# Two dense tiles of the latent tokens in one PSUM bank: layer 1's mixer of a hybrid backbone kernel

## The chip, the cores and the metric

The kernel runs on one core of one Trainium2 chip. The metric is the device time of one launch in microseconds (us), the median of several runs. Three runs of the kernel before took 2468.72, 2463.49 and 2462.4 us: median 2463.49.

## What is computed

Two layers work on 256 latent tokens and 256 context tokens of width 1024, in fp32. Each layer normalises, projects its input, runs three mixers side by side (centred pooling, a bidirectional RWKV-7 recurrence, neighbourhood attention), projects each mixer's output, gates and sums the three, and projects again; then comes a feed-forward part, dense in layer 0 and with 8 experts in layer 1. In the last layer the context is only read: it needs its keys, values and recurrence inputs, but no outputs. The reference, cut to the mixer:

```python
def token_mixer(h, hc, w_in, ..., need_ctx_out):
    zp, zr, zq, zk, zv, zg = jnp.split(h @ w_in, splits, axis=-1)
    zrc = hc @ w_in[:, OFF_RWKV:OFF_Q]                  # last layer: of the context only these
    zkc, zvc = jnp.split(hc @ w_in[:, OFF_K:OFF_GATE], 2, axis=-1)
    ...
    branches = (pool_branch(zp, ...), rwkv_readout(wkv, ...), nat)
    y = gated_merge(branches, zg, w_branch, w_out)

def gated_merge(branches, gate_pre, w_branch, w_out):
    proj = jnp.einsum('btnc,ncd->btnd', jnp.stack(branches, axis=2), w_branch)
    gates = jax.nn.sigmoid(gate_pre.reshape(B, T, N_BRANCH, D_MODEL))
    return jnp.sum(gates * proj, axis=2) @ w_out
```

## The kernel before

Activations lie transposed, channels on the 128 partitions, tokens along the free axis: the context's 256 columns, then the latent 256. A *dense tile* is 128 output channels: one tile of weights (128 x 1024, or 128 x 512 for a branch projection) is loaded, ScalarE casts it to a high part `whi` (L205), VectorE subtracts to get a low part `wlo` (L209), and TensorE adds up three products for each of 8 (or 4) blocks of the input: `whi` with the input's high part, `whi` with its low part, `wlo` with its high part, 24 (or 12) matmuls into one PSUM tile (L249 to L251, or L499 to L501 where other work is woven in between). There are two `whi`/`wlo` buffers for the mixer's weights, so the cast for the tile after next waits until TensorE has used up the first.

A dense tile's PSUM comes from `mm`, which in the mixer has two banks of 512 fp32 columns (`self.psum(f"m{l}", sm=2, mm=2)`). In layer 0 all tiles have 512 columns, context and latent. In layer 1 (`full` is False) the tiles that the context doesn't need, pooling inputs, r, the recurrence's gate input `glo`, queries, the 24 output gates, the branch projections and the output projection, have only the latent 256; such a tile takes a bank and uses half of it:

```python
def bank(self, tag, n):
    p, bufs = self.banks[tag]
    t = p.tile([128, 512], F32, name=tag, tag=tag, bufs=bufs)
    return t[:, :n]
```

A bank goes to the next tile when the last instruction that reads it is done. These readers *empty* a tile: a ScalarE copy for pooling inputs (L1205), for queries and keys (L1085) and values (L1116); ScalarE with a scale and then VectorE twice for r, k, v and `glo`, which are shifted by a token both ways (L531, L533, L535); ScalarE's Tanh for a gate (L1257); VectorE for a branch projection, multiplied with its gate (L1269 in the woven part, L1246 in the last merge); VectorE's residual for the output projection (L1521). They are given a high priority (`leave()`).

Order: up to the end of the recurrence's readout TensorE's order is written out. `Order.run` takes pieces of several lanes (attention, triangular solves, norms) by due times, and dense tiles fill what is left. TensorE runs its instructions in that order, whatever is ready. The other engines' order is set by the scheduler. In layer 1 the mixer has four stages:

- the front: k, r, v, pooling, queries, keys, values of w_in, and the recurrence's operands;
- attention (`attend`), the triangular solves (`solve`) and, as filling, `pool_merge`: for f = 0 to 7 a gate tile (24 matmuls), then a merge tile (12 matmuls) of the pooling branch; then four `early_gate` tiles, gates of the recurrence's branch;
- the chunk scan (`core`), 8 chunks in both directions, with `dense` as filling: per f a gate tile of the recurrence's branch (for f = 4 to 7; the first four are there), a gate tile and a merge tile of the attention branch;
- the last merge of the recurrence's branch (`merge_branch`, 8 tiles of 12) and the output projection (8 tiles of 24, with routing products L1646 for the experts). Here the scheduler orders TensorE too.

Then come the experts, fed from HBM.

Of the kernel before, what the change touches and what calls it, by code (L numbers as in the profile page):

```python
# [54 lines left out]
class Order:  # L55
# [4 lines left out]
    def __init__(self):  # L60
        self.now, self.lanes = 0.0, []
# [42 lines left out]
class Builder:  # L104
    def __init__(self, ctx, tc, I, out, dbg=None):
        self.ctx, self.tc, self.nc, self.I, self.out = ctx, tc, tc.nc, I, out
        self.dbg = dbg or {}
        self.nlo, self.lo_first = 0, 0
        self.pre, self.ahead = [], []
        self.raws, self.parted, self.pin = (), (), False  # L110
        self.late_lo = ()
        self.nraw = self.nparts = 0
        self.banks = {}
        self.norm_banks = ExitStack()
        self.sq = self.rs = None
        self.hw = 512
        self.cpool = ctx.enter_context(tc.tile_pool(name="consts", bufs=1))
        self.dram = ctx.enter_context(tc.tile_pool(name="dr", bufs=1, space=DRAM))
        nc = self.nc
        cst = self.cpool.tile([128, C_N], F32, name="cst")  # L120
        nc.sync.dma_start(cst, I["cst"])
        self.cst = cst
        self.ident = cst[:, C_ID:C_ID + 128]
        self.mask = cst[:, C_MSK:C_MSK + 128]
        self.i2 = cst[:, C_I2:C_I2 + 64]
        self.ob = cst[:, C_OB:C_OB + 128]
        self.ones = cst[:, C_ON:C_ON + 128]
        self.tiny = ctx.enter_context(tc.tile_pool(name="tiny", bufs=6))
        hb = self.cpool.tile([40, 4, 128], F32R, name="hb")
        with tc.tile_pool(name="hb0", bufs=1) as hp:  # L130
            hb0 = hp.tile([40, 4, 128], F32, name="hb0")
            nc.sync.dma_start(hb0, I["heads"])
            nc.vector.tensor_copy(hb, hb0)
        self.hb = hb
        self.vec = []
        for l in range(2):
            v = self.cpool.tile([128, V_N], F32, name=f"vec{l}")
            nc.sync.dma_start(v, I["vec"][l])
            self.vec.append(v)
        self.mod = [[None] * 6 for _ in range(2)]  # L140
# [35 lines left out]
        return t[:, :n]  # L176

    def mm(self, n=512):
        return self.bank("mm", n)

    def sm(self, n=512):
        return self.bank("sm", n)
# [1090 lines left out]
    def mixer(self, l, x, full, xnew, done=lambda: None):  # L1273

        nc, tc = self.nc, self.tc
        n = 512 if full else 256
# [4 lines left out]
        n = 512 if full else 256  # L1281
        self.bonus, self.gain = ([self.dram.tile([128, n], F32, name=f"{a}{l}{c}") for c in range(4)] for a in ("bon", "gan"))
        ex = ExitStack()
        P = lambda name, bufs, **k: tc.tile_pool(name=f"{name}{l}", bufs=bufs, reuse_waits="tile", **k)
        ex.enter_context(self.psum(f"m{l}", sm=2, mm=2))
        self.sp_small = ex.enter_context(P("small", 1))
        self.lo_mod, self.lo_pool, self.lo_first = 2, 0, 0
        self.raws, self.parted = (self.wa, self.wa) + tuple(ex.enter_context(P("w", 1)) for _ in range(l)), (self.wa,)
# [372 lines left out]
    def moe(self, l, x):  # L1661
        nc, tc, I = self.nc, self.tc, self.I
        ident = self.ident
        with ExitStack() as ex:
            P = lambda name, bufs, **k: ex.enter_context(
                tc.tile_pool(name=f"{name}m", bufs=bufs, reuse_waits="tile", **k))
            ex.enter_context(self.psum("e", mm=4))
            self.lo_mod, self.lo_pool = 8, 0
            self.nlo, self.lo_first = 0, 0
            self.nparts, self.parted = 0, (P("w", 2), self.wa)  # L1670
# [464 lines left out]
```

## Time and profile before

| | |
|---|---|
| median of three runs | 2463.49 us |
| the profiled execution | 2462.03 us, span 2459.8 us |
| TensorE (PE) busy | 2310.2 us, 94% of the span |
| weight loads (PEld) busy | 1851.1 us, 75% |
| VectorE (DVE) busy | 1894.2 us, 77% |
| ScalarE (ACT) busy | 1281.2 us, 52% |
| GpSimd (POOL) busy | 95.4 us, 4% |
| DMA | 514.29 MB, mean 209 GB/s |

Times of the rows below count from the span's start. A busy matmul is not one at its peak, since matmuls overlap. "Idle before" is the time for which an engine had nothing running ahead of the instruction, and what ended it; a wait for several things is put down to the last. The mixer of layer 1 ends at about 1645 us, the experts take the rest.

### The profile page before, as it was taken

The page shows a single profiled execution, that of the slowest core. Times are in us where ns is not written, and L with a number is a line of the kernel's source. Part 1 is how long each engine was busy: PE and PEld are TensorE (multiplying, and loading weights), DVE is VectorE, ACT ScalarE, POOL GpSimd, SP SyncE. Part 2 cuts the span into 40 slices and gives each one's busy share as a digit, 9 for nine tenths or more (in the row PEclk, how much of TensorE's full clock was granted, in tenths as well). Part 3 has the DMA queues.
Part 4 walks back from the last instruction along what each step waited for, and adds up shares of the span by engine and source line. Part 5 has one row for each costly group of instructions (what it writes and reads, how often), then busy time and mean ns, then how long its engine had stood idle before and what let it go on. Part 6 is the DMA issues. An engine that isn't in the chain of part 4 may idle for free. (4 is left out here: it accounts for less than half of the span.)

```text
span 2459.8 us, 40024 instructions
## 1 busy us (share of the span) xinstructions
PE 2310.2 (94%) x15206; PEld 1851.1 (75%) x15206; DVE 1894.2 (77%) x3133; ACT 1281.2 (52%) x1882; POOL 95.4 (4%) x94
## 2 busy tenths in 40 slices
PE   6899998999899999999889898889999999999998
PEld 4667667777578888777667687678888888888876
DVE  4795776787857666765885867769999999889897
ACT  4563654222333322234654543258777777777775
POOL 0000000000001221120000000000000000000000
PEclk9999998999999999999989989989999999999999
DMA  6274223564424444762663345576999999999995
GB/s 254 87 199 124 91 90 92 173 179 151 150 86 137 152 140 138 265 207 78 167 166 107 112 130 172 168 273 221 366 339 346 362 359 337 348 360 338 358 345 194
DMA packets 227594, 514.29 MB, mean 209 GB/s; under 512 B 70875, under 2 KB 105051, under 8 KB 226243
## 3 DMA queue, kind: packets, MB, share of 16 engines
q1 hardware_dynamic: 227394, 511.67, 61.7%
q8 instruction: 121, 1.98, 0.3%
q14 instruction: 79, 0.64, 0.1%
HBM read 484.79 MB, written 26.74 MB: 208 GB/s over the span
## 5 line engine op out<-in xcount | busy, mean ns | idle before, releaser
L205 ACT CAST whi<-wraw 128x1024 fp32r<-128x1024 f32 (+2 forms) x753 | 755.0, 1020 | 601.1 <-DMA wraw<-in_ffn 185.9
L209 DVE TENSOR_TENSOR wlo<-wraw,whi 128x1024 fp32r<-128x1024 f32 (+1 forms) x719 | 838.9, 1193 | 169.8 <-ACT whi L205 158.6
L499 PE MATMUL mm<-h,whi 128*128 128x512 f32 (+1 forms) x864 | 344.9, 399 | 24.1 <-ACT u L1085 6.7
L501 PE MATMUL mm<-h,wlo 128*128 128x512 f32 (+1 forms) x864 | 318.1, 368 | 7.6 <-DVE wlo L209 7.6
L500 PE MATMUL mm<-h,whi 128*128 128x512 f32 (+1 forms) x864 | 318.9, 369 | 4.9 <-DVE h L484 4.9
L1853 PE MATMUL mm<-whi,xh 128*128 128x512 f32 (+1 forms) x768 | 289.2, 377 | 0.0
L1854 PE MATMUL mm<-whi,xl 128*128 128x512 f32 (+1 forms) x768 | 288.1, 375 | 0.0
L1855 PE MATMUL mm<-wlo,xh 128*128 128x512 f32 (+1 forms) x768 | 281.5, 376 | 1.3 <-DVE wlo L209 1.3
L499 PEld LDWEIGHTS mm<-h,whi 128*128 128x128 f32 x864 | 171.0, 198 | 76.4 <-issue 24.6
L501 PEld LDWEIGHTS mm<-h,wlo 128*128 128x128 f32 x864 | 171.0, 198 | 37.5 <-DVE wlo L209 11.3
L500 PEld LDWEIGHTS mm<-h,whi 128*128 128x128 f32 x864 | 171.9, 199 | 31.5 <-DVE h L484 8.0
L251 PE MATMUL mm<-h,wlo 128*128 128x512 f32 (+1 forms) x448 | 171.4, 383 | 2.2 <-DVE wlo L209 2.0
L250 PE MATMUL mm<-h,whi 128*128 128x512 f32 (+1 forms) x448 | 170.3, 381 | 0.7 <-DVE h L484 0.7
L249 PE MATMUL mm<-h,whi 128*128 128x512 f32 (+1 forms) x448 | 169.7, 381 | 1.4 <-ACT whi L205 1.4
L1855 PEld LDWEIGHTS mm<-wlo,xh 128*128 128x128 f32 x768 | 144.0, 188 | 29.2 <-DVE wlo L209 1.9
L1854 PEld LDWEIGHTS mm<-whi,xl 128*128 128x128 f32 x768 | 144.4, 188 | 27.1
L1853 PEld LDWEIGHTS mm<-whi,xh 128*128 128x128 f32 x768 | 144.6, 188 | 26.4
L1882 PE MATMUL mm<-wlo,hh 128*128 128x512 f32 x352 | 139.6, 397 | 0.8 <-DVE wlo L209 0.8
L1881 PE MATMUL mm<-whi,hl 128*128 128x512 f32 x352 | 139.1, 395 | 0.0
L1880 PE MATMUL mm<-whi,hh 128*128 128x512 f32 x352 | 138.8, 394 | 0.0
L209 POOL TENSOR_TENSOR wlo<-wraw,whi 128x1024 fp32r<-128x1024 f32 (+1 forms) x34 | 79.4, 2337 | 760.7 <-DMA wraw<-in_ffn 426.6
L251 PEld LDWEIGHTS mm<-h,wlo 128*128 128x128 f32 x448 | 84.5, 189 | 22.3 <-DVE wlo L209 3.3
(378 smaller groups left out, 3751.9 us busy)
## 6 DMA issues: line engine op xcount, KB each, us to landing
wraw<-in_moe SPq DMA_DIRECT2D x516, 512.0 KB, 5.5
wraw<-in_w_in SPq DMA_DIRECT2D x108, 512.0 KB, 3.7
wraw<-in_w_mod SPq DMA_DIRECT2D x72, 512.0 KB, 4.6
wraw<-in_ffn SPq DMA_DIRECT2D x60, 512.0 KB, 3.7
rakbv<-std SPq DMA_DIRECT2D x32, 640.0 KB, 5.3
wraw<-in_w_branch SPq DMA_DIRECT2D x48, 256.0 KB, 2.7
u<-in_w_mod SPq DMA_DIRECT2D x48, 256.0 KB, 4.3
std<-st SPq DMA_DIRECT2D x16, 640.0 KB, 5.2
```

Source lines behind the costliest of these rows:

```text
L205: nc.scalar.copy(hi, src)
L209: return e.tensor_tensor(lo, src, hi.bitcast(F32), op=OP.subtract)
L249: nc.tensor.matmul(ps, wh, xh, start=i == 0, stop=False)
L250: nc.tensor.matmul(ps, wh, xl, start=False, stop=False)
L251: nc.tensor.matmul(ps, wl, xh, start=False, stop=i == n - 1)
L499: nc.tensor.matmul(ps, wh, xh, start=i == 0, stop=False)
L500: nc.tensor.matmul(ps, wh, xl, start=False, stop=False)
L501: nc.tensor.matmul(ps, wl, xh, start=False, stop=i == n - 1)
L1853: nc.tensor.matmul(ps, xh[:, k0 + k], hi[:, w], start=k0 + k == 0, stop=False)
L1854: nc.tensor.matmul(ps, xl[:, k0 + k], hi[:, w], start=False, stop=False)
L1855: nc.tensor.matmul(ps, xh[:, k0 + k], lo[:, w], start=False, stop=k0 + k == 7)
L1882: nc.tensor.matmul(y, hid[k][0], lo[:, w], start=False, stop=k == KF - 1)
```

## The change

`mm` gets a mode, `pairs`, switched on for the mixer of layer 1 and off for the experts. With it a tile of at most 256 columns takes a new bank only every second time: the first takes columns 0 to 255, the next one columns 256 to 511 of the same bank. A tile of more than 256 columns takes a bank of its own and ends an open pair.

```diff
--- before.py
+++ after.py
@@ -106,6 +106,7 @@
         self.ctx, self.tc, self.nc, self.I, self.out = ctx, tc, tc.nc, I, out
         self.dbg = dbg or {}
         self.nlo, self.lo_first = 0, 0
+        self.pairs, self.half = False, None
         self.pre, self.ahead = [], []
         self.raws, self.parted, self.pin = (), (), False
         self.late_lo = ()
@@ -176,7 +177,15 @@
         return t[:, :n]
 
     def mm(self, n=512):
-        return self.bank("mm", n)
+        if n > 256 or not self.pairs:
+            self.half = None
+            return self.bank("mm", n)
+
+        if self.half is None:
+            self.half = t = self.bank("mm", 512)
+            return t[:, :256]
+        t, self.half = self.half, None
+        return t[:, 256:]
 
     def sm(self, n=512):
         return self.bank("sm", n)
@@ -1283,6 +1292,7 @@
         ex = ExitStack()
         P = lambda name, bufs, **k: tc.tile_pool(name=f"{name}{l}", bufs=bufs, reuse_waits="tile", **k)
         ex.enter_context(self.psum(f"m{l}", sm=2, mm=2))
+        self.pairs, self.half = not full, None
         self.sp_small = ex.enter_context(P("small", 1))
         self.lo_mod, self.lo_pool, self.lo_first = 2, 0, 0
         self.raws, self.parted = (self.wa, self.wa) + tuple(ex.enter_context(P("w", 1)) for _ in range(l)), (self.wa,)
@@ -1665,6 +1675,7 @@
             P = lambda name, bufs, **k: ex.enter_context(
                 tc.tile_pool(name=f"{name}m", bufs=bufs, reuse_waits="tile", **k))
             ex.enter_context(self.psum("e", mm=4))
+            self.pairs, self.half = False, None
             self.lo_mod, self.lo_pool = 8, 0
             self.nlo, self.lo_first = 0, 0
             self.nparts, self.parted = 0, (P("w", 2), self.wa)
```

In the new file the lines of the mixer stand nine or ten further down: L499 becomes L508, L1257 becomes L1266, L1269 becomes L1278, L1646 becomes L1656.

What the change does to the order shows in three places. The number of a buffer tells which allocation it is; `[waits ...]` names the engine whose count the instruction waits for. First, TensorE in the attention stage, where merge 1 ends and gate 2 begins; then two score products of attention (`sm`) and one of the recurrence's output gate. Before:

```order
L500 MATMUL mm_12013<-u2_11799,whi_12009 128x256
L501 MATMUL mm_12013<-u2_11798,wlo_12010 128x256
L499 MATMUL mm_12040<-h_10011,whi_12036 128x256 [waits Activation_49]
L500 MATMUL mm_12040<-h_10012,whi_12036 128x256
L501 MATMUL mm_12040<-h_10011,wlo_12037 128x256 [waits DVE_49]
L1150 MATMUL sm_12045<-u_11571,u_11150 128x512
L1150 MATMUL sm_12046<-u_11571,u_11150 128x512 [waits Activation_49]
L764 MATMUL sm_12073<-u_11859,g2_10116 128x256 [waits DMAHW3_49,Activation_49]
L499 MATMUL mm_12040<-h_10020,whi_12036 128x256
```

and now:

```order
L509 MATMUL mm_12007<-u2_11795,whi_12003 128x256
L510 MATMUL mm_12007<-u2_11794,wlo_12004 128x256
L508 MATMUL mm_12007<-h_10011,whi_12030 128x256 [waits DVE_49]
L509 MATMUL mm_12007<-h_10012,whi_12030 128x256
L510 MATMUL mm_12007<-h_10011,wlo_12031 128x256
L1159 MATMUL sm_12038<-u_11567,u_11148 128x512
L1159 MATMUL sm_12039<-u_11567,u_11148 128x512 [waits Activation_49]
L773 MATMUL sm_12066<-u_11855,g2_10116 128x256 [waits DMAHW3_49,Activation_49]
L508 MATMUL mm_12007<-h_10020,whi_12030 128x256
```

The order is the same; gate 2 now goes to the bank of merge 1, and its first matmul waits for VectorE, where it waited for ScalarE. Its third matmul has no wait for `wlo` of its own any more.

Second, ScalarE at the start of the scan: casts of weights, and the Tanh of the last early gate and of the first gate of `dense` (`u_13434` before, `u_13420` now). Before:

```order
L205 CAST whi_13469<-wraw_13467 128x512
L1257 ACTIVATE gp_13066<-mm_13073 128x256
L205 CAST whi_13491<-wraw_13489 128x1024
L1257 ACTIVATE u_13434<-mm_13441 128x256
L205 CAST whi_13551<-wraw_13549 128x512
```

and now:

```order
L214 CAST whi_13455<-wraw_13453 128x512
L1266 ACTIVATE gp_13053<-mm_13013 128x256
L214 CAST whi_13476<-wraw_13474 128x1024
L1266 ACTIVATE u_13420<-mm_13427 128x256
L214 CAST whi_13536<-wraw_13534 128x512
```

Nothing moves here: the cast for the tile after next stands ahead of the Tanh in both.

Third, TensorE in the output projection, at the end of its first tile (f=0, then the routing product `nl` of f=0). Before:

```order
L250 MATMUL mm_15712<-h_15676,whi_15706 128x256 [waits DVE_49]
L251 MATMUL mm_15712<-h_15675,wlo_15707 128x256
L250 MATMUL mm_15750<-h_15676,whi_15744 128x256
L251 MATMUL mm_15750<-h_15675,wlo_15745 128x256
L249 MATMUL mm_15712<-h_15702,whi_15706 128x256 [waits Activation_49]
L249 MATMUL mm_15750<-h_15702,whi_15744 128x256
L250 MATMUL mm_15712<-h_15703,whi_15706 128x256 [waits DVE_49]
L251 MATMUL mm_15712<-h_15702,wlo_15707 128x256
L250 MATMUL mm_15750<-h_15703,whi_15744 128x256
L251 MATMUL mm_15750<-h_15702,wlo_15745 128x256
L1646 MATMUL nl_15475<-xl_10270,rt1_15463 8x256 [waits DVE_49]
L1646 MATMUL nl_15475<-xl_10272,rt1_15463 8x256 [waits DVE_49]
```

and now:

```order
L258 MATMUL mm_15684<-h_15674,whi_15678 128x256 [waits Activation_49]
L259 MATMUL mm_15684<-h_15675,whi_15678 128x256 [waits DVE_49]
L260 MATMUL mm_15684<-h_15674,wlo_15679 128x256
L1656 MATMUL nl_15451<-xl_10270,rt1_15439 8x256 [waits DVE_49]
L258 MATMUL mm_15684<-h_15493,whi_15716 128x256
L259 MATMUL mm_15684<-h_15494,whi_15716 128x256
L260 MATMUL mm_15684<-h_15493,wlo_15717 128x256
L258 MATMUL mm_15684<-h_15519,whi_15716 128x256
L259 MATMUL mm_15684<-h_15520,whi_15716 128x256
```

Before, f=0 (`mm_15712`) and f=1 (`mm_15750`) are worked on in turn; now the whole of f=0 stands ahead of the first matmul of f=1, and so does its routing product, which waits for VectorE.

## Rows read from the trace of the kernel before

**Rows 1.** Windows by stage: length, then busy (count) of each engine.
```profile
core 0: us, PE busy (x) PEld busy (x) DVE busy (x) ACT busy (x) POOL busy (x), PEclk, DMA share, GB/s
1186.00:1317.00 131.00, 111.88 (x788) 89.32 (x788) 101.03 (x173) 72.55 (x130) 3.94 (x14) 0.91 0.62 162
1317.00:1455.00 138.00, 122.74 (x1252) 102.90 (x1251) 100.92 (x234) 70.36 (x129) 0.31 (x1) 0.89 0.35 108
1455.00:1592.00 137.00, 122.36 (x1942) 107.97 (x1940) 98.81 (x226) 47.34 (x100) 0.00 (x0) 0.98 0.57 170
1592.00:1645.00 53.00, 47.75 (x324) 40.25 (x324) 34.17 (x70) 25.05 (x51) 0.00 (x0) 0.91 0.75 280
1660.00:2459.00 799.00, 788.01 (x3818) 653.76 (x3816) 722.03 (x743) 603.58 (x675) 1.81 (x1) 1.00 0.90 329
```

**Rows 2.** TensorE's waits, 1317 to 1455: us in total, times, longest.
```profile
PE mm L501 <- DVE wlo L209: 5.2, 8, 1.4
PE mm L499 <- ACT u L1257: 2.8, 3, 1.3
```

**Rows 3.** TensorE's waits, 1455 to 1592.
```profile
PE sm L877 <- issue: 4.6, 4, 1.9
PE sm L877 <- DVE Gr L883: 3.3, 4, 1.0
```

**Rows 4.** TensorE's waits, 1186 to 1317.
```profile
PE mm L499 <- ACT u L1085: 6.7, 2, 4.2
PE mm L499 <- ACT z L1205: 5.3, 2, 3.1
```

**Rows 5.** Timeline, first gate and merge of the scan: start, length, instruction.
```profile
1453.64 0.41 PE L501 MATMUL mm<-h,wlo 128*128 128x256 f32 x1
1453.85 0.41 PE L499 MATMUL mm<-u,whi 128*128 128x256 f32 x1
1453.92 1.05 ACT L205 CAST whi<-wraw 128x1024 fp32r<-128x1024 f32 x1 [2.73 <-issue]
...
1454.88 0.38 ACT L1257 ACTIVATE u<-mm 128x256 f32<-128x256 f32 x1
```

**Rows 6.** Timeline, last gate and merge of the scan.
```profile
1563.55 0.28 PE L499 MATMUL mm<-u,whi 128*128 128x256 f32 x1
...
1564.20 0.38 ACT L1257 ACTIVATE u<-mm 128x256 f32<-128x256 f32 x1
```

**Rows 7.** Timeline, attention: from merge 1 to gate 2.
```profile
1333.56 0.38 PE L499 MATMUL mm<-h,whi 128*128 128x256 f32 x1 [0.62 <-ACT u L1257]
...
1334.61 0.38 PE L501 MATMUL mm<-h,wlo 128*128 128x256 f32 x1 [0.55 <-DVE wlo L209]
...
1334.84 0.42 DVE L1269 SCALAR_TENSOR_TENSOR u<-u,mm 128x256 f32<-128x256 f32 x1
```

**Rows 8.** Timeline, attention: gate 0 starts; the glo tile is emptied.
```profile
1321.25 0.39 PE L499 MATMUL mm<-h,whi 128*128 128x256 f32 x1
...
1323.31 0.48 DVE L535 SCALAR_TENSOR_TENSOR u<-mm,vec,u 128x255 f32<-128x255 f32 x1
```

**Rows 9.** Timeline, attention: early gate 3 starts; early gate 2 is emptied.
```profile
1428.45 0.28 PE L499 MATMUL mm<-h,whi 128*128 128x256 f32 x1
...
1430.27 0.39 PE L501 MATMUL mm<-h,wlo 128*128 128x256 f32 x1 [1.42 <-DVE wlo L209]
...
1432.26 0.37 ACT L1257 ACTIVATE gp<-mm 128x256 f32<-128x256 f32 x1
```

**Rows 10.** Timeline, output projection: f=0 and f=1 are emptied; f=2 starts.
```profile
1620.20 0.88 DVE L1521 SCALAR_TENSOR_TENSOR xl<-mm,mod,xl 128x256 f32<-128x256 f32 x2 [1.84 <-PE mm L251]
...
1621.70 0.39 PE L249 MATMUL mm<-h,whi 128*128 128x256 f32 x1
```

**Rows 11.** Two windows of the attention stage; columns as in rows 1.
```profile
1411.00:1413.30 2.30, 1.43 (x9) 1.22 (x10) 2.25 (x7) 2.30 (x6) 0.00 (x0) 1.00 0.00 0
1413.40:1416.70 3.30, 3.30 (x24) 2.76 (x23) 1.35 (x2) 0.65 (x2) 0.00 (x0) 0.50 0.74 264
```

## Prediction

> **What bounds the kernel now.** I read the stage windows first, since the edit lives in one stage, layer 1's mixer, and what it is worth there decides; then the waits of TensorE in that stage; then the order of instructions of both programs; last the timeline at the places that the order marks. The windows [rows 1] cut the mixer into its front (1186 to 1317 us), attention with the pooling merges (to 1455), the chunk scan with the attention merges (to 1592) and the last merge with the output projection (to 1645). TensorE is busy 111.88 of 131, 122.74 of 138, 122.36 of 137 and 47.75 of 53 us: it is the bound, with 5 to 19 us of idle per stage. The experts behind it keep TensorE busy 788.01 of 799 us, so they can't make up what the mixer loses: a microsecond there is a microsecond at the end.
>
> How much of that idle time is the lack of a free `mm` bank, which is what the change speaks to? In attention TensorE waited 2.8 us in all, three times, for ScalarE to empty a gate tile (L1257) [rows 2]; in the scan no `mm` wait is among the long ones [rows 3]; in the front it waited 6.7 us for L1085 and 5.3 us for L1205 [rows 4]. That is 14.8 us, the most that more tiles in flight could give.
>
> **What the change does in the order.** A pair shares one bank, and in the built program the first matmul of the right half carries a wait for the instruction that empties the left half (first place in the order: before, gate f+1 waited for ScalarE, for a tile two back; now for VectorE, for merge f's L1269, numbered L1278 in the new file). So not four tiles are in flight but two, one per bank, and the neighbour in a pair is the tile just behind, not two behind. I count the second halves of the mixer: 4 in the front, 10 in attention, 10 in the scan, 4 in the last merge, 4 in the projection. In the front three of the four wait for the same emptying as before, since there the scheduler already put the tile into the bank just emptied (the other was held by a 512-column tile); so the 12.0 us of [rows 4] stay, and one wait is new. 29 new waits in all. TensorE works in order, so all behind the waiting matmul on it waits too: scores, transposes and the scan's products, and with them the VectorE and ScalarE work that those feed.
>
> A rule speaks to this. The Trainium skill's page "PSUM — Partial Sum Buffer", section "PSUM bank collisions raise a hardware error", says that the hardware neither arbitrates nor stalls when two engines touch one bank and quadrant, even at different addresses, and that PSUM is to be guarded by bank, not by address. No run here shows a collision; by that rule no schedule could drop these waits.
>
> **The price of one wait**, from the timeline of before: the end of the emptying instruction, plus 0.05 us to the first matmul, less the time at which the second tile started, less the idle time behind it that goes because its own cause has passed meanwhile.
> - Scan, first: the gate's last matmul starts at 1453.64, the merge's first at 1453.85, and the gate's Tanh runs 1454.88 to 1455.26 [rows 5]. The merge would start at 1455.31: 1.46 us later. The Tanh isn't late by chance: ScalarE first casts the weights of the tile after next (1.05 us from 1453.92), into the buffer that the gate's last matmuls free, and this order is the same in both programs (second place). 0.44 us of later idle (a wait for VectorE's `wlo`) goes: 1.0.
> - Scan, last: 1563.55 against a Tanh that ends at 1564.58 [rows 6]: 1.1.
> - Between them eight more, read likewise: 1.7, 1.2, 1.1, 1.0, 1.8, 1.5, 0.7, 0.8. Ten together: 11.7. TensorE also idled 4.6 us before L877, four times, for nothing that the profile shows [rows 3]; late in the scan that may be a `rakbv` transfer that would then arrive in time. I take 2 off: 9.7.
> - Attention, gate behind merge (five): merge 1 is emptied by L1269, 1334.84 to 1335.26, and gate 2 would start at 1335.31. In before it started at 1333.56, ran two matmuls and then stood until 1334.61 for `wlo` [rows 7]. `wlo` is ahead of L1269 on VectorE, so that stand goes: 0.70 later, plus the two matmuls, 0.95. The five: 1.0, 0.95, 0.6, 0.6, 0.9, together 4.1.
> - Attention, the others: gate 0 behind the glo tile, whose last reader L535 ends at 1323.79, against a start at 1321.25 [rows 8]; three `rh` products (0.43 us each) now stand ahead of it, 1.3 left. Merges 6 and 7 behind their gates 0.8 and 1.1. Early gate 1: 1.9. Early gate 3: its neighbour is emptied at 1432.63, it started at 1428.45 and lost 1.42 us at 1430.27 anyway [rows 9]: 2.5. Together 7.6, attention 11.7.
> - Front: one wait at the scan's price, 1.5.
> - Last merge and projection have no hand-written order. There the right half can't run beside the left any more: projection tiles f=0 and f=1 were interleaved (third place in the order) and both emptied in 1620.20 to 1621.08, with f=2 at 1621.70 [rows 10]. Now f=1 starts when f=0 is emptied, about 1620.7, and its 24 matmuls at some 0.12 us (0.21 at half clock [rows 5]) take 2.9: f=2 comes at 1623.5, 1.8 late. Three more pairs at about 0.6 (emptying 0.48, less the routing product between): 1.8. The first pair of the merge loses its overlap likewise, twelve matmuls and 0.42: 1.9. Together 5.5.
>
> No instruction is added or removed; the DMAs are the same and only shift with their buffers.
>
> Sum: 1.5 + 11.7 + 9.7 + 5.5 = 28.4 us of waiting.
>
> **The clock.** TensorE's granted clock fell from its level of 2.4 GHz (share 1.00) to 1.2 (0.50) behind idle times no longer than these: in 1411.0 to 1413.3 it was busy 1.43 of 2.30 us at 1.00, and in 1413.4 to 1416.7 it ran at 0.50 [rows 11]. Such a stretch of 3.3 us does 1.65 us of full-speed work and so costs 1.65. But the scan, with 14.6 us of idle time in 137, kept a mean of 0.98 [rows 1]. 29 idle times of about 1 us bring some: with three, 5.0 us. None is the lower bound, one behind every second wait (14, 23 us) the upper.
>
> So 28.4 + 5.0 = 33.4. The profiled execution took 2462.0 us (span 2459.8), 1.5 below the median of 2463.5; on the median that is **2497 us**. Bounds: the emptying can come sooner than I read it, for TensorE's standing gives the other two engines time to catch up (the latest, at 1432.63 [rows 9], sat behind other ScalarE work). With 0.5 us left per wait, 29 make 15: 2478. With nothing absorbed (5 us in the scan and behind `wlo` more) and eight slow stretches, 28.4 + 5 + 13 = 46, and a few more for knock-on waits: 2515.
>
> **The rivals.**
> - *The halves do work side by side* (the other side: faster). If the right half were written while the left is emptied, the 14.8 us of [rows 2, 4] would go at most: 2449. For it: these waits are real, and they sit on the engine that bounds. The Trainium skill's page "Perfetto Trace Analysis", section "Optimization Strategy", says that the same gap repeating on the engine that should be saturated can mean too little PSUM for the next tile; [rows 4] look like that, and by it the change would be the cure. Against: the waits stand in the built order, and in the front the same tiles wait for the same emptyings. It decides only if most second halves start before the left is emptied. 4 in 100.
> - *Nothing to measure*: gains in the front and losses behind cancel, 2460 to 2470. 5 in 100.
> - *The waits are there but short*: eviction is prompt once TensorE stands, about 0.35 us left for each, no clock loss: 10 us, 2473. For it: L1521 runs at once behind its tile [rows 10]; against: the cast ahead of each Tanh [rows 5] waits for the same matmuls as the Tanh. 9 in 100.
> - *The clock pays most*: a slow stretch behind two of three waits, 20 x 1.65 = 33 more: 2525. For it [rows 11]; against, the scan's 0.98. 9 in 100.
>
> **Numbers.** The likeliest, 2484 to 2512 around 2497, has 73 in 100. The range 2478 to 2515 leaves out the faster and same cases, part of the short waits and most of the clock case. A change of under 0.3%, 7.4 us, can't be told from none here: faster 0.04, same 0.05, slower 0.91.
>
> **What would show it.** In the profile after, the waits list of TensorE in attention and scan gets new entries: gate matmuls of L499 (there L508) waiting for L1269's successor L1278, and merge matmuls waiting for the Tanh L1266, about ten each way, mean near 1.3 us, before absorption. The `wlo` waits of [rows 2] shrink. The projection's f=0 and f=1 come one after the other. The expert stage keeps its length, about 799 us from its first weights. More half-clock stretches in 1317 to 1592. Wrong would be: no such entries; or entries that sum to under 15 us; or the extra time in the experts.

## The result, and the profile after

The changed kernel took 2494.95 us (median of 4 runs: 2492.51, 2491.53, 2497.40, 2497.76), the kernel before beside it 2462.97. Ratio 1.0123, 95% interval 1.0099 to 1.0147: slower. 2497 was predicted, 2478 to 2515 the range.

The profiled execution took 2492.51 us (span 2490.3, 30.5 more than before). The windows of the changed kernel that answer to [rows 1], cut at the same tiles:

```profile
1191.40:1322.00 130.60, 112.11 (x788) 89.92 (x788) 100.93 (x173) 72.48 (x131) 3.94 (x14) 0.91 0.61 163
1322.00:1473.10 151.10, 120.23 (x1252) 102.34 (x1251) 102.61 (x235) 71.52 (x129) 0.31 (x1) 0.90 0.33 100
1473.10:1618.80 145.70, 125.73 (x1941) 110.21 (x1939) 98.38 (x225) 47.21 (x99) 0.00 (x0) 0.96 0.52 156
1618.80:1676.10 57.30, 48.89 (x323) 41.51 (x323) 35.17 (x70) 25.21 (x51) 0.00 (x0) 0.88 0.74 272
1691.20:2489.50 798.30, 788.29 (x3820) 653.97 (x3818) 722.01 (x743) 604.15 (x675) 1.81 (x1) 1.00 0.90 329
```

Length less PE busy is TensorE's idle time. The four mixer windows grew from 459.0 to 484.7 us, by 25.7: idle time by 23.5 (54.27 to 77.74), busy time by 2.2 (404.73 to 406.96, for the same matmuls, so this is the granted clock). The experts kept their length. The rest of the 30.5 lies ahead of all that was changed: the first window starts 5.4 us later than its counterpart, which the experiments show to be variation between executions.

TensorE's new waits, in the list of waits (us in all, times, longest), first attention, then the scan. One of the scan's ten, 1.35 us at 1471.98, falls into the first window:

```profile
PE mm L508 <- DVE u L1278: 8.9, 5, 2.4
PE mm L508 <- ACT whi L214: 5.8, 1, 5.8
PE mm L508 <- ACT u L1266: 5.4, 3, 2.7
PE sm L773 <- ACT pr L1169: 4.6, 3, 2.1
PE ch L837 <- issue: 2.6, 1, 2.6
PE mm L508 <- ACT gp L1266: 1.7, 1, 1.7
...
PE mm L510 <- DVE wlo L218: 0.2, 1, 0.2
```

```profile
PE mm L508 <- ACT u L1266: 6.7, 7, 1.5
PE sm L886 <- DVE Gr L892: 3.0, 4, 1.0
PE sm L886 <- issue: 2.2, 2, 1.4
PE mm L508 <- DVE u L1278: 2.2, 2, 1.6
```

The entries of the pairs (all of L508, 19 in number) sum to 30.7 us: five gates of attention and two of the scan behind the VectorE instruction that empties the merge just ahead (L1278), eight merges and two gates of the scan behind the Tanh of the gate just ahead (L1266), and two early gates. The 5.8 us put down to a cast are one of the early gates: the Tanh behind that cast is the true last condition (below). The waits for `wlo`, 5.2 us in [rows 2], shrank to 0.2, and L877's 4.6 for nothing visible [rows 3], now L886, to 2.2.

In the timeline one place of each kind. Merge 1 to gate 2 (answers to [rows 7]), and the first gate and merge of the scan ([rows 5]):

```profile
1344.19 0.42 DVE L1278 SCALAR_TENSOR_TENSOR u<-u,mm 128x256 f32<-128x256 f32 x1
1344.66 0.39 PE L508 MATMUL mm<-h,whi 128*128 128x256 f32 x1 [2.37 <-DVE u L1278]
...
1470.60 1.05 ACT L214 CAST whi<-wraw 128x1024 fp32r<-128x1024 f32 x1 [2.80 <-issue]
1471.55 0.38 ACT L1266 ACTIVATE u<-mm 128x256 f32<-128x256 f32 x1
...
1471.98 0.38 PE L508 MATMUL mm<-u,whi 128*128 128x256 f32 x1 [1.35 <-ACT u L1266]
```

The merge starts 0.05 us behind the Tanh, and the Tanh runs behind the cast, as the prediction read it; the wait is 1.35 us where 1.46 was worked out.

The largest wait is early gate 3's (answers to [rows 9]). Early gate 2's last matmul starts at 1439.79:

```profile
1439.08 2.10 ACT L826 COPY V<-svT 32x1024 f32<-32x1024 f32 x2 [1.47 <-DVE svT L823]
...
1442.13 0.58 ACT L1180 COPY pt<-ch 128x512 f32<-128x512 f32 x1
1442.60 2.09 ACT L826 COPY V<-svT 32x1024 f32<-32x1024 f32 x2
1444.72 1.05 ACT L214 CAST whi<-wraw 128x1024 fp32r<-128x1024 f32 x1
1445.67 0.38 ACT L1266 ACTIVATE gp<-mm 128x256 f32<-128x256 f32 x1
1445.82 0.58 PE L508 MATMUL mm<-h,whi 128*128 128x256 f32 x1 [5.75 <-ACT whi L214]
```

ScalarE has two pairs of the triangular solver's copies (L826) and the attention's copies (L1180) in front of the cast and the Tanh, and works without a pause from 1439.08 on. Before, only one pair of these copies (there L817) stood ahead of that Tanh, the other behind it, and gate 3 ran beside all that:

```profile
1429.17 2.11 ACT L817 COPY V<-svT 32x1024 f32<-32x1024 f32 x2 [1.84 <-DVE svT L814]
1431.30 1.06 ACT L205 CAST whi<-wraw 128x1024 fp32r<-128x1024 f32 x1
1432.26 0.37 ACT L1257 ACTIVATE gp<-mm 128x256 f32<-128x256 f32 x1
1432.54 1.03 ACT L817 COPY V<-svT 32x1024 f32<-32x1024 f32 x1
```

So at this place the change moved ScalarE's own order: a pair of copies, 2.1 us, came ahead of the Tanh. The traces show this order in every run below with pairs at the early gates (e2, e3, e7), and without them only in e8. The prediction had compared ScalarE's two orders at the start of the scan alone.

In the front nothing was lost: the waits of [rows 4] stand at 5.1 us for L1205 (now L1214) and 7.4 for L1085 (now L1094), in which the one new wait of 1.29 is counted, and idle time went from 19.1 to 18.5. That is this one execution; the fronts of the experiments vary (below). The projection's f=0 and f=1 come one after the other: f=0's matmuls run 1643.21 to 1647.44, f=1's 1648.55 to 1651.62. In the last merge the granted clock fell. Its window before, then after:

```profile
1596.80:1614.20 17.40, 15.25 (x97) 13.53 (x98) 12.83 (x32) 7.65 (x16) 0.00 (x0) 0.88 0.58 204
```

```profile
1623.60:1643.20 19.60, 16.21 (x96) 15.05 (x97) 14.48 (x34) 8.42 (x17) 0.00 (x0) 0.76 0.61 214
```

### The profile page after: what moved, and what is told of

Its sections match the earlier page's. It is cut to its first block, busy times and chain, and to the rows that moved or that the text cites. A ratio compares the mean times of both kernels' runs of the same rounds, so it can differ in the third digit from the quotient of the medians.

```text
span 2490.3 us, 40018 instructions
## 1 busy us (share of the span) xinstructions
PE 2320.3 (93%) x15206; PEld 1862.3 (75%) x15206; DVE 1897.9 (76%) x3133; ACT 1283.1 (52%) x1882; POOL 95.6 (4%) x94
## 5 line engine op out<-in xcount | busy, mean ns | idle before, releaser
L508 PE MATMUL mm<-h,whi 128*128 128x512 f32 (+1 forms) x864 | 347.6, 402 | 42.8 <-DVE u L1278 11.1
L508 PEld LDWEIGHTS mm<-h,whi 128*128 128x128 f32 x864 | 173.2, 200 | 95.5 <-issue 26.1
L509 PEld LDWEIGHTS mm<-h,whi 128*128 128x128 f32 x864 | 173.9, 201 | 32.5 <-DVE h L493 8.8
L510 PEld LDWEIGHTS mm<-h,wlo 128*128 128x128 f32 x864 | 172.3, 200 | 29.7 <-DVE wlo L218 3.3
L258 PEld LDWEIGHTS mm<-h,whi 128*128 128x128 f32 x448 | 85.1, 190 | 21.7 <-ACT whi L214 1.5
```

The lines of the kernel that those rows point to most:

```text
L258: nc.tensor.matmul(ps, wh, xh, start=i == 0, stop=False)
L508: nc.tensor.matmul(ps, wh, xh, start=i == 0, stop=False)
L509: nc.tensor.matmul(ps, wh, xl, start=False, stop=False)
L510: nc.tensor.matmul(ps, wl, xh, start=False, stop=i == n - 1)
```

## The experiments

My theory: the whole cost is the wait for the emptying of the tile just ahead, stage by stage. The rivals: half banks cost something by themselves; the clock pays; losses are knocked on from one stage to the next.

All stages are read from the timelines, between the starts and ends of the same tiles: front (first 256-column tile to the end of the last 512-column one), attention (to the first merge of the scan), scan (to the end of its last merge), readout, last merge (8 tiles), projection (8 tiles). *Mixer* is the start of the first 256-column tile to the start of the first expert tile. These come from the one profiled execution of each run, the ratio from all its executions. In us:

| run | front | attention | scan | readout | last merge | projection | mixer | ratio to before, 95% |
|---|---|---|---|---|---|---|---|---|
| before | 157.8 | 136.2 | 112.5 | 30.4 | 17.4 | 28.9 | 497.9 | |
| after | 157.5 | 149.5 | 118.9 | 32.7 | 19.6 | 31.1 | 523.9 | 1.0123 (1.0099 to 1.0147) |
| e1 | 167.9 | 134.6 | 114.6 | 30.1 | 17.5 | 29.5 | 508.7 | 1.0044 (1.0025 to 1.0062) |
| e2 | 157.6 | 149.3 | 121.3 | 31.4 | 19.2 | 31.1 | 524.5 | 1.0102 (1.0077 to 1.0128) |
| e3 | 157.5 | 148.3 | 114.7 | 31.8 | 18.0 | 29.2 | 514.1 | 1.0066 (1.0039 to 1.0093) |
| e4 | 157.1 | 135.5 | 121.3 | 31.4 | 17.6 | 29.6 | 507.2 | 1.0024 (1.0001 to 1.0047) |
| e5 | 155.2 | 131.8 | 114.8 | 31.5 | 20.2 | 31.1 | 499.2 | 1.0009 (0.9989 to 1.0029) |
| e6 | 161.4 | 131.7 | 111.4 | 29.9 | 19.0 | 29.0 | 496.9 | 1.0006 (0.9989 to 1.0023) |
| e7 | 160.9 | 148.9 | 115.9 | 33.1 | 19.6 | 31.2 | 524.1 | 1.0102 (1.0060 to 1.0145) |
| e8 | 159.5 | 144.4 | 118.2 | 33.1 | 18.0 | 29.6 | 517.3 | 1.0102 (1.0062 to 1.0142) |
| e9 | 157.7 | 134.2 | 111.7 | 31.5 | 18.2 | 28.8 | 496.7 | 0.9993 (0.9975 to 1.0010) |
| e10 | 161.9 | 141.8 | 117.8 | 31.5 | 19.5 | 31.1 | 518.2 | 1.0090 (1.0058 to 1.0121) |

Where a stage has the waits of before it still varies: attention 131.7 to 136.2, scan 111.4 to 114.8. TensorE's idle time (length less busy time) sets most of the clock's part in this aside. "With pairs" means here that two tiles in a row share a bank, which they don't in e1 and e9. In attention the idle time is 29.8 to 30.9 us with pairs (after, e2, e3) and 14.8 to 17.9 without (before, e1, e4, e5, e6, e9); in the scan 13.9 to 14.8 with pairs (after, e2, e4, e10) and 7.5 to 9.2 without (before, e1, e3, e5, e6, e9). The mean granted clock differs little between the two groups: attention 0.90 with pairs and 0.89 to 0.94 without, scan 0.97 to 1.00 with and 0.97 to 0.98 without. So in these two stages the clock, one of the rivals, doesn't carry the loss.

**e1 and e9: the neighbour two tiles back.** Two banks are opened, then their right halves follow in the same order; in e9 from attention on only.

```diff
-        if self.half is None:
-            self.half = t = self.bank("mm", 512)
-            return t[:, :256]
-        t, self.half = self.half, None
+        if self.half is None:
+            self.half = [], []
+        new, old = self.half
+        if len(new) < 2 and not old:
+            new.append(self.bank("mm", 512))
+            if len(new) == 2:
+                self.half = [], new[:]
+            return new[-1][:, :256]
+        t = old.pop(0)
         return t[:, 256:]
```

> Two banks are opened with their left halves, then their right halves follow in the same order: the neighbour in a bank is the tile two back, not the tile just behind. Theory (the cost is the wait for the emptying of the tile just behind, nothing else): the waits are again those of the kernel before, and the mixer, from the start of its first 256-column tile to the start of the first expert tile, takes 498 us as before (1159.80 to 1657.68), against 524 after (1164.98 to 1688.87); total 2457 to 2470, ratio 0.998 to 1.003. Rival (half banks cost by themselves: a half that is written while its neighbour is read, or a lower clock): the mixer stays above 510 us and the total above 2475.

Measured: mixer 508.7, between the two. Attention and all behind it are as before, but the front lost 10 us, which neither side had expected. The list of waits in the front has a new entry (L513 is L499 of before, L549 its L535):

```profile
PE mm L513 <- DVE s L549: 20.9, 2, 10.6
```

The timeline shows the first of the two:

```profile
1194.72 0.74 DVE L549 SCALAR_TENSOR_TENSOR s<-mm,vec,s 128x510 f32<-128x510 f32 x1
...
1195.60 0.55 PE L513 MATMUL mm<-h,whi 128*128 128x256 f32 x1 [10.62 <-DVE s L549]
```

Of the two banks one held a 512-column tile that VectorE empties late, the other a narrow one that ScalarE empties sooner. Before, the next narrow tile took the second. Here that bank was kept for its right half, so the tile went to the first and waited. Of the 12.0 us of [rows 4] only 2.5 were left beside the new 20.9, so the front lost 10 and not 21. That reading was tested:

> As run e1 (the neighbour in a bank is two tiles back), but with halves only from attention on; the front has whole banks. Theory (in e1 the 10 us were the front's alone, where the pool could no longer choose the bank that comes free first; half banks cost nothing by themselves): mixer 495 to 502 us, total 2458 to 2470. Rival (halves side by side cost a little everywhere): mixer 505 or more.

Measured: mixer 496.7, ratio 0.9993. The list of waits in e9's attention repeats [rows 2] entry for entry, with eight waits of 5.2 us and three of 2.8 (L515 is L501, L513 is L499):

```profile
PE mm L515 <- DVE wlo L223: 5.2, 8, 1.4
PE mm L513 <- ACT u L1271: 2.8, 3, 1.3
```

So half banks cost nothing by themselves that could be measured. The cost is which tile's emptying the next matmul stands behind.

**e2: the left half twice.**

```diff
-        return t[:, 256:]
+        return t[:, :256]
```

> Both tiles of a pair get the left half of the bank, so they overwrite the same 256 columns. Theory (no two tiles of a bank are in flight together anyway): the same time as the changed kernel, mixer 521 to 527 us, total 2488 to 2500. Rival A (the halves do work side by side in part, and that saves something): mixer over 529 us, total over 2502. Rival B (right halves cost something by their place in the bank): mixer under 515, total under 2485.

Measured: mixer 524.5, total 2490.91, as the theory has it. Overwriting the same columns costs no more than taking the other half: the two tiles of a pair are never in flight together. That is what the Trainium skill's page "PSUM — Partial Sum Buffer", section "PSUM bank collisions raise a hardware error", leads to: PSUM is guarded by bank. The order carries these waits; no run shows a collision. No run shows either whether the program would wait as well if each half were a tile of its own: here both halves belong to one tile that takes a whole bank.

**e3, e4, e5: one stage at a time.** The same line stands at different places: at the mixer's start (off in e4 and e5), before `dense()` (off in e3, on in e4) and before the last merge (off in e4, on in e5):

```diff
+        self.pairs, self.half = not full, None      # or: False, None
```

> Pairs in the front and in attention alone, off from the chunk scan on. Theory (each stage pays for its own waits, and the sum adds up): 13.2 us by the forecast's terms (1.5 front, 11.7 attention) and 12.7 by the trace after (front -0.4, from there to the first merge of the scan +13.1): mixer 509 to 513 us, total 2472 to 2480. Rival (what attention loses pushes the scan, or what the scan lost was pushed by attention): mixer over 517 or under 505. On what the layers ahead of the change took longer in the profile after (5.2 us to the mixer's first 256-column tile): theory, variation from run to run, so 0 to 6 us here without pattern; rival, it belongs to the change, and shows here as 5 us again.

> Pairs in the chunk scan and the readout alone. Theory (each stage pays for itself): 9.7 us by the forecast's term, 8.7 by the trace after (shift 18.1 at the first merge of the scan, 26.8 at the first tile of the last merge): mixer 505 to 509 us, total 2468 to 2476. Rival (the scan's loss is knocked on from attention): mixer under 502. Rival (clock: its half-clock stretches come with the waits and cost as much again): mixer over 514.

> Pairs in the last merge and the output projection alone. Theory: 5.5 us by the forecast's term, 4.4 by the trace after; mixer (first 256-column tile to first expert tile) 502 to 504 us against 498 before, total 2464 to 2472. Rival (the last stage of the changed kernel was late because the scan ahead of it was): mixer 497 to 500.

Measured: e3's attention 148.3, e4's scan 121.3, e5's last merge 20.2 and projection 31.1, each like the changed kernel's own stage, and the stages without pairs like before's. Losses are local and add up. Means with pairs (after, and e3, e4, e5, e10 where they apply) less means without (before, e1, e3, e4, e5, e9 likewise; e10's attention is left out): attention 148.9 - 134.5 = 14.4, scan 119.3 - 113.7 = 5.7, last merge 19.77 - 17.74 = 2.0, projection 31.1 - 29.2 = 1.9, together 24.0 of the mixer's 26.0 (e2, e6 and the exchanges e7 and e8 are not counted). Readout, 31.9 - 31.1, and front, 159.0 (157.5, 157.5, 161.9) - 157.0, lie within what unchanged stages vary by. In e5 the two stages lost 5.0 us, but its attention, unchanged, ran 4.4 us shorter than before's, so that the mixer grew by only 1.3 and the total says nothing. By the ranges on record e5's mixer, 499.2, is the rival's (497 to 500); its two stages, late with no loss ahead of them, decide for the theory. e4's mixer lies in the theory's range. e3's mixer was 514.1 where 509 to 513 was expected; 3.6 of its 16.2 us lie in the scan and readout, which it doesn't change.

**e6: more tiles really in flight**, in whole banks that stand idle in the front and in the last stage.

```diff
-        return self.bank("mm", n)
+        if n > 256 or not self.tags:
+            return self.bank("mm", n)
+        self.nmm += 1
+        return self.bank(self.tags[self.nmm % len(self.tags)], n)
...
+            self.tags = () if full else ("ch", "mm")      # front
...
+        self.tags = () if full else ("sm", "mm")          # last merge and projection
```

> The kernel before, no halves: in layer 1's front the 256-column tiles go in turn to the ch and the mm banks, in the last merge and projection in turn to the sm and the mm banks, whole banks that stand idle there. So more tiles are really in flight in these two stages. Theory A (the front's 12 us of waits for L1205 and L1085 are a lack of banks): front, 157.8 us before, takes 146 to 152; total 2451 to 2458. Theory B (the banks only move the wait: the head norm's chain on VectorE, 6.8 us of wait before L290, ends when it did): front 155 to 158, total 2460 to 2466. In the last merge and projection (46.3 us before, waits of about 2 us, nearly all for casts) both expect a gain of at most 1 us.

Measured: mixer 496.9, nothing gained. The 12 us of [rows 4] are gone, and in the front's list of waits stand others (L503 is L499, L539 is L535, L294 is L290):

```profile
PE sm L294 <- DVE rs L271: 6.1, 1, 6.1
PE mm L503 <- DVE s L539: 5.6, 2, 3.2
PE ch L673 <- DVE st L657: 3.5, 2, 2.6
```

The front took 161.4 us for 157.8, and the last merge and projection 48.0 for 46.3. The front waits for VectorE, with more banks too: theory B, though its figure was 155 to 158. The mixer came out level because attention, unchanged, ran 4.5 us shorter than before's. The prediction had weighed a sentence of the Trainium skill's page "Perfetto Trace Analysis", section "Optimization Strategy", by which repeated gaps can mean too little PSUM. These gaps were of that kind, for they went when banks were added, and yet that was no cure: the front gained nothing, for the waits for VectorE shown above took their place.

**e7 and e8: the Tanh ahead of the cast**, in the changed kernel and in the kernel before. The last two matmuls of a tile change places, and so the cast can start no sooner than the Tanh:

```diff
+            if i == n - 1 and ps.shape[-1] <= 256:
+                nc.tensor.matmul(ps, wl, xh, start=False, stop=False)
+                nc.tensor.matmul(ps, wh, xl, start=False, stop=True)
+            else: ...
```

> The changed kernel, with the last two matmuls of a woven 256-column tile exchanged, so that the last one reads whi: the cast into that buffer can then start no sooner than the Tanh that empties the tile, and ScalarE runs the Tanh first. Theory (1.05 us of each wait behind a gate tile is the cast that runs ahead of its Tanh): 12 pairs of the mixer have a gate on the left, 4 in attention and 8 in the scan; each wait falls by 1.05 us or to nothing, by the waits seen after about 9 us together; mixer 512 to 518 us instead of 523.9, total 2483 to 2491. Rival (the wait is the emptying's own way, matmul to ScalarE to TensorE, and other work on ScalarE): mixer over 520.

> The kernel before with the same exchange. Theory (there the Tanh has a whole tile of time, so that it may come late): mixer 495 to 500 us against 497.9, total 2458 to 2468; the 2.8 us of waits for L1257 in attention may go, and the later casts may add as much in waits for wlo. Rival (the exchange speeds up or slows down the mixer by itself, so that run e7 tells nothing of the pairs): mixer off by 5 us or more.

Measured: the waits fell as the theory has it, the time did not. e7's mixer, 524.1, lies in the rival's range (over 520), and e8's is off by far more than the rival's 5 us. The scan's first merge in e7 (L1270 is the Tanh):

```profile
1471.91 0.38 ACT L1270 ACTIVATE u<-mm 128x256 f32<-128x256 f32 x1 [3.11 <-PE mm L511]
1472.19 1.04 ACT L214 CAST whi<-wraw 128x1024 fp32r<-128x1024 f32 x1
...
1472.35 0.39 PE L508 MATMUL mm<-u,whi 128*128 128x256 f32 x1 [0.47 <-ACT u L1270]
```

1.35 us became 0.47, so the cast was 0.9 of it; the scan's waits for its Tanh went from 8.1 us (the 6.7 above and the 1.35) to

```profile
PE mm L508 <- ACT u L1270: 3.0, 6, 0.6
```

and the scan from 118.9 to 115.9 us. The four such waits of attention went from 11.4 to 6.8 us, which makes 9.7 us in all where about 9 was expected. But casts that start later make `wlo` late: in attention the `wlo` waits went from 0.2 us to 5.0. (The front took 160.9 us, within the 157.5 to 161.9 of fronts with the changed kernel's code.) In the kernel before the exchange cost 19.4 us of mixer, which the rival had named and I had not believed. Its attention:

```profile
PE mm L505 <- DVE wlo L209: 12.1, 9, 2.4
PE sm L768 <- ACT pr L1164: 4.6, 3, 2.1
PE mm L499 <- ACT whi L205: 2.7, 3, 1.2
```

where [rows 2] has 5.2 for `wlo`. By e8's own warning e7's total says nothing about the size of the cast's share; the single waits do. With the exchange in both, pairs cost 524.1 - 517.3 = 6.8 us in the two profiled executions; the medians, 2490.06 and 2486.42, differ by 3.6, and the ratios are the same, so this cost is not clear of noise.

**e10: the early gates by themselves.**

```diff
         def early_gate(f):
+            self.pairs, self.half = False, None
...
         fill = dense()
+        self.pairs, self.half = not full, None
```

> The changed kernel, but the four early gates at the end of attention have whole banks. Theory (early gates 1 and 3 waited 1.66 and 5.75 us for the Tanh of the gate just ahead, the latter behind ScalarE's copies for the solver; the wait of 2.61 us at L837 behind it grew from 1.17 for the same reason): these go but for the 1.4 us for wlo that the kernel before has there; from the front's end to the first merge of the scan 141 to 145 us, where the changed kernel took 149.5 and the kernel before 136.2; mixer 515 to 520, total 2481 to 2491. Rival (ScalarE and VectorE are behind there whatever the banks do, so another wait takes the place): that stretch over 147 us, mixer over 521.

Measured: attention 141.8 us, mixer 518.2, total 2488.31, as the theory has it. The waits of 5.8 and 1.7 us are gone from the list of attention, L837's went from 2.6 to 0.8, and `wlo` came back:

```profile
PE mm L508 <- DVE u L1278: 8.9, 5, 2.4
PE mm L508 <- ACT u L1266: 5.4, 3, 2.7
PE sm L773 <- ACT pr L1169: 4.6, 3, 2.1
PE mm L510 <- DVE wlo L218: 1.7, 2, 1.4
```

On ScalarE the second pair of the solver's copies stands behind the Tanh again, as before. Two of attention's ten pairs made 7.7 of the 13.3 us that it lost. The front's 161.9, with the code of the changed kernel, is variation (157.5 there). No version beat the kernel before; e6 and e9 equal it.

## Why the prediction was right, and where it was not

The mechanism was right: two tiles in flight and not four, each right half behind the emptying of the tile just ahead, with the entries in the waits list that were named, the experts unchanged, f=1 behind f=0. e2 and e9 show it from both sides. The list of waits has 19 such entries, mean 1.6 us, for about twenty of 1.3. The terms, idle time and clock by the windows:

| term | predicted | measured |
|---|---|---|
| front | 1.5 | -0.6 |
| attention | 11.7 | 14.2 (15.6, less the scan's 1.35) |
| scan and readout | 9.7 | 6.7 (5.3 and that 1.35) |
| last merge and projection | 5.5 | 3.2 |
| clock | 5.0 | 2.2 (busy time) |
| sum | 33.4 | 25.7 |

- *Front*: the new wait was there, 1.29 us for 1.5, but two others shrank: the wait for L1085 of 4.22 us, which lies ahead of it, became 3.54, and that for the head norm behind it, 6.79 us, became 5.94. I took nothing off for that.
- *Attention*: early gate 3 was mis-sized, 2.5 (some 2.7 by its own method) for 5.75 gross. Less the 1.42 us for `wlo` that went, and with 1.44 more at L837, it is 5.8. I took ScalarE's order and the time of the Tanh in before [rows 9] as given. But in the changed kernel a second pair of the solver's copies, 2.1 us, stands ahead of that Tanh. The other terms came near: gate 0's products ahead of it waited 1.7 us for 1.3, merges 6 and 7 lost 1.5 (4.0 less 2.5 that went) for 1.9, early gate 1 1.7 for 1.9, and 0.5 at L1168 went. The five gates behind merges waited 8.9 us gross, and 3.9 us of waits for `wlo` and L1257 beside them went, with 1.0 at L764: 4.1, as predicted.
- *Scan*: its ten waits sum to 10.3 us where the prediction read 11.7 (its ten figures add to 11.9, with 0.44 for `wlo` already taken off). That the other engines catch up while TensorE stands, the lower bound's reason, would explain it; no run shows that. And more came back than the 2 us taken off: 2.4 at L877, 1.2 at L912 and 0.9 for `wlo`, less 1.0 by which other waits grew.
- *Last merge and projection*: idle time grew by 3.2 where 5.5 was reckoned. With 1.1 of busy time, which belongs to the clock's term, the stages grew by 4.4 us in all (2.2 each).
- *Clock*: by busy time 2.2 us and not 5: 3.4 in the scan's window, 1.1 in the last, 0.2 in the front, and 2.5 less in attention, where 15.6 us of new idle time left the mean at 0.90 for 0.89. Of the scan window's 3.4 us 2.8 lie in the readout, which has no pairs (busy 21.4 us before, 24.2 after, and 21.4 to 24.2 in the experiments, without a pattern); the scan itself ran at 0.99 for 0.98. So the waits of attention and scan brought no slower clock, where the prediction had put slow stretches behind them, and no run shows its 5.0. Only the last merge was slower with pairs (granted clock 0.76 to 0.81 in after, e2, e5, e7 and e10, 0.85 to 0.88 in the runs without; 0.80 in e6, which gives it other banks). The rival with 20 such stretches was far off. The prediction also has two upper ends for the clock, 14 stretches in one place and eight in the other.
- *The total* was nearer than its parts. 2497 - 2462.97 is 34 us for 32 measured, but the mixer lost 26. e2, which waits at the same places, has a ratio of 1.0102, about 25 us, inside the first result's interval (its medians differ by 28): the change is probably worth about 26 us, and some 6 of the 32 are what executions differ by. That the forecast was 7 us too high in the mixer stays hidden in the total. That the total came within 2 us of the forecast is luck.

## What to carry to other kernels

More tiles in a bank are not more tiles in flight when the wait is kept per bank: look in the built order at which instruction the second tile waits for, and on the emptying engine at what stands ahead of that instruction, at every such place and in both programs. On the engine that bounds, a wait on the tile just ahead costs the emptying plus whatever stands ahead of it on its engine, here a 1 us cast, once a run of copies; with the neighbour two tiles back (e9) it cost nothing. And read such waits as a sum over stages, with the waits behind them that go.

## What was not expected of the hardware

Ahead of the first 256-column tile of layer 1 all twelve kernels run the same matmuls. That tile began 1159.8 us into the span before, 1165.0 after, and in the ten experiments between 1154.0 (e8) and 1163.8 (e5). These are the windows up to it, of before and of after:

```profile
0.00:1159.80 1159.80, 1083.35 (x6920) 831.04 (x6921) 807.65 (x1615) 442.40 (x767) 89.04 (x77) 0.97 0.47 148
```

```profile
0.00:1165.00 1165.00, 1091.31 (x6921) 838.70 (x6922) 809.17 (x1615) 442.64 (x767) 89.19 (x77) 0.97 0.47 147
```

The same matmuls kept TensorE busy 8.0 us longer, so between these two the clock made the difference, though both means round to 0.97. It isn't the only cause: in e5, which reached that tile 4.0 us later than before, TensorE was busy 1083.65 us, as long as before, and idle for longer. Attention without pairs shows the same on a smaller scale: 136.2 us at a granted clock of 0.89 before, 131.8 at 0.94 in e5.

```profile
1317.60:1453.80 136.20, 120.94 (x1241) 101.18 (x1240) 100.92 (x234) 68.69 (x126) 0.31 (x1) 0.89 0.35 107
```

```profile
1319.00:1450.80 131.80, 113.93 (x1240) 95.33 (x1240) 100.72 (x234) 68.63 (x126) 0.31 (x1) 0.94 0.36 110
```

What makes the clock and the idle time differ from one execution to the next was not found. These differences are the reason why single stages, and not totals, were compared here.
